# Three units of a recurrent mixer emitted side by side in slots, instead of one chain after another

## The chip, the cores and the metric

The kernel runs on one core of one Trainium2 chip. The metric is the device time of one execution in microseconds (us); smaller is better. Engines are named as the profile names them: PE is the matrix engine (PEld its weight loads), DVE the vector engine, ACT the scalar engine, POOL the GpSimd engine, SP the engine whose queue issues nearly all DMAs. L990 is line 990 of the kernel before; in the changed kernel the same statements stand some lines earlier.

## The reference, cut to what matters

One transformer layer over 256 latent tokens and 256 context tokens of width 2048: a SwiGLU block, a token mixer, a second SwiGLU block, each followed by a layer norm. The change is in the mixer alone. Half of the mixer is a gated MLP over 128-token chunks; the other half is a delta-rule recurrence, run in both directions over 16 heads of 64 channels:

```python
p_x = h_x @ w_in; p_c = h_c @ w_in
def step(s, inp):                       # per token, per head; s is 64 x 64
    r_t, v_t, w_t, k_t, a_t, b_t = inp
    sa = einsum('bhvk,bhk->bhv', s, a_t)
    s = s * w_t + sa[..., None] * b_t + v_t[..., None] * k_t
    return s, einsum('bhvk,bhk->bhv', s, r_t)
y = group_norm(ys[0] + ys[1]); out = (y + bonus) * g
out_x = concatenate([out, gmlp_mix(gm_x)]) @ w_out
```

## The kernel before, in words

**Units.** The recurrence is cut into 16 units: eight row tiles `t` of two heads each (128 channels), times two directions `d`. Each unit has 512 tokens in eight chunks of 64. Inside a chunk the recurrence is turned into small matrix products: `prep` builds decays and masked 64x64 products, `small_inverse` and `inverse` invert a triangular matrix per head and chunk, and `solve` applies the inverse and then walks the eight chunks in series: each step is two products `pS` (L1020), one DVE update `S` (L1023), and for the last four chunks two products `py` (L1010) and one DVE addition (L1011).

**Three calls per unit.** The loop calls `finish(u)` (that is `solve`, L930 to L1024, and a group norm), then `inverse(u + 1)` (L860 to L924), then for every second unit `epilogue`, then `begin(u + 2)` (`prologue` for a new row tile, `prep`, `small_inverse`, and `bonus`). No unit needs another one's result, apart from tiles that both directions of a row tile share: the three calls of one turn of the loop are independent of each other, but each stands in the program behind the one before it.

**The broadcast.** `small_inverse` puts 16x16 blocks into `a16` (eight DVE instructions, L842), writes them to DRAM (`scr`, L846), reads them back spread over the partitions (`abc`, 1 MB, L848), and then runs 15 dependent pairs of a product (`a<-x,abc`, L855) and a sum (`x<-a`, L856) on DVE. Both DMAs are issued on SP, whose queue also carries all weight loads.

**The filler.** The large products (`gemm`, `gmlp_v`, `wout`; L309 to L311, three matmuls per step of 128 channels) do not depend on the unit in hand. They stand in a `queue` of generators. `tick(w)` and `pad(w)`, called behind the small products, add `w * pace` to a debt, and once the debt has reached `BURST = 5` steps (`pad`: at once) emit large products until it is paid. `PACE` gives the weight of each place; `UNIT` is their sum over a unit, and `pace` is set per unit from the work that is left.

**What orders the instructions.** A list scheduler puts the emitted instructions into one queue per engine when the program is built: it follows the order of emission, and takes a later instruction first where its own reckoning says that the earlier one isn't ready. On the chip each of these queues is worked off in that fixed order.

Of the kernel before, what the change touches and what calls it, by code (L numbers as in the profile page):

```python
# [38 lines left out]
PACE = dict(pz=0.6, px=0.5, pt=2.8, pak=1.0, pX=0.7, pR=0.7, pu=1.1, pg=1.0, pS=0.83, rb=6, yn=0, bk=3)  # L39
# [14 lines left out]
def tile_layer(ctx: ExitStack, tc: tile.TileContext, x, c, ctx_in, c_ctx, w_ada, b_ada, ln_g, ln_b,  # L54
# [574 lines left out]
    UNIT = sum(n * PACE[k] for k, n in dict(pz=1, px=8, pt=3, pak=4, pX=8, pR=8, pu=8, pg=12, pS=6, rb=0.5, yn=0.5, bk=1).items())  # L629
# [10 lines left out]
    ahead = [0]  # L640

    def prefer(n):
        ahead[0] = n
        return tc.high_priority(offset=n) if n else nullcontext()
# [8 lines left out]
    def pad(w):  # L653

        owed[0] += w * pace[0]
        with tc.high_priority(offset=-ahead[0]) if ahead[0] else nullcontext():
            while queue and owed[0] > 0:
                owed[0] -= advance()

    def drain(gen=None):  # L660
        while queue and (gen is None or gen in queue):
            owed[0] -= advance()
        owed[0] = max(owed[0], -8.0)
# [57 lines left out]
    def prep(t, d, k, r, kk, vt, ups, kdx):  # L721
# [8 lines left out]
        tick(PACE["pz"])  # L730
# [43 lines left out]
        if d == 0:  # L774
            nc.scalar.copy(kdx, kd[:, T:W2])
        else:
            nc.gpsimd.tensor_tensor(kdx, kdx, kd[:, T:W2], op=ALU.add)

# [4 lines left out]
        for half in (1, 0):  # L783
            w = L * (1 + half)
            if half:
                pad(PACE["bk"])
            pxs = [ps_s("px") for _ in range(2)]
            for q in range(2):
                for g in range(2):
# [9 lines left out]
                    tick(PACE["px"])  # L799
# [9 lines left out]

        rhs = held("rhs", (P, 4, 2, 2, 64))  # L810
# [5 lines left out]
        tick(PACE["pt"])  # L816
        nc.scalar.copy(rhs[:, :, :, 1, :], pt.rearrange("p (g h c) -> p g h c", g=4, h=2))
        for q in range(2):
            pt = ps_s("pt")
            for g in range(4):  # L820
                nc.tensor.transpose(pt[:, P * g:P * g + P], bk[q][:, g].rearrange("p m s -> p (m s)"), ident)
            tick(PACE["pt"])
            nc.scalar.copy(fl(bkt[:, q]), pt)
        pt = ps_s("pak")
        for g in range(4):
# [5 lines left out]
            tick(PACE["pak"])  # L831
        nc.scalar.copy(rhs[:, :, :, 0, :], pt.rearrange("p (g h c) -> p g h c", g=4, h=2))
        return dict(wn=wn, rt=rt, aa=aa, arm=arm, rhs=rhs, bkt=bkt)

    def small_inverse(d, s):

        a16 = own("a16", (P, 8, 16))
        for b in range(4):
            for q in range(2):
# [9 lines left out]
                            scr.rearrange("(g s) c -> g (s c)", g=8).unsqueeze(1).to_broadcast([8, 16, 2048]))  # L849
        x = own("x16", (P, 8, 16), bufs=2)  # L850
        nc.scalar.copy(x, i16.unsqueeze(1).to_broadcast([P, 8, 16]))
        sub = own("a16", (P, 8, 16))
        for i in (range(1, 16) if d == 0 else range(14, -1, -1)):
            r = slice(0, i + 1) if d == 0 else slice(i, 16)
            nc.vector.tensor_tensor(sub[:, :, r], x[:, :, r], abc[:, r, :, i].rearrange("p s j -> p j s"), op=ALU.mult)  # L855
            nc.vector.tensor_reduce(x[:, :, i], sub[:, :, r], axis=AX.X, op=ALU.add)  # L856
        s["x16"] = x

    def inverse(d, s):

        aa = s["aa"]

# [5 lines left out]
        nc.vector.transpose(Rt, R1)  # L868
        pX = ps_v("pX")
        for i in range(8):  # L870
# [4 lines left out]
            if i % 2:  # L875
                tick(PACE["pX"])
        Z = own("Z", (P, 8, 32))
        nc.vector.tensor_tensor(Z, pX[:, 0:256].rearrange("p (i t) -> p i t", t=32),
                                ml[d].unsqueeze(1).to_broadcast([P, 8, 32]), op=ALU.mult)
        pR = ps_v("pR")  # L880
        for i in range(8):
# [3 lines left out]
            if i % 2:  # L885
                tick(PACE["pX"])
# [7 lines left out]
        fa, fb = (0, 32) if d == 0 else (32, 0)  # L894
        pX = ps_v("pX2")
        for i in range(8):
# [4 lines left out]
            if i % 2:  # L901
                tick(PACE["pR"])
        Z = own("Z", (P, 8, 32))
        for q in range(2):
# [4 lines left out]
            else:  # L909
                nc.vector.tensor_copy(Z[sb], pz)  # L910
        pR = ps_v("pR2")
        for i in range(8):
# [3 lines left out]
            if i % 2:  # L916
                tick(PACE["pR"])
# [9 lines left out]
    def solve(d, s, vt, y):  # L927
# [7 lines left out]
        for half in range(2):  # L935
            pu = ps_v("pu")
            for g in range(2):
                for h in range(2):
# [5 lines left out]
                    tick(PACE["pu"])  # L944
# [4 lines left out]
            nc.scalar.copy(uv[1][64:128, g2], puv[64:128, :, :, 0, :])  # L949

# [9 lines left out]

        pgs = [ps_v("pg") for _ in range(2)]
        pqs = [ps_v("pq"), ps_s("pq")]
        HS = [slice(64 * h, 64 * h + 64) for h in range(2)]

        def pq_at(q, g, m):
            return pqs[q][:, 128 * g + 64 * m:128 * g + 64 * m + 64]

        for g in range(4):
# [4 lines left out]
            if g >= 2:  # L973
                for q in range(2):
                    for h in range(2):
                        nc.tensor.matmul(pq_at(q, g - 2, 0)[HS[h]], ua[HS[q], g, h, :], arm[HS[q], q, h, g - 2, :],
                                         start=True, stop=True)
        tick(6 * PACE["pg"])
        for q in range(2):
# [4 lines left out]
            for g in range(2):  # L984
                for h in range(2):
                    nc.tensor.matmul(pq_at(q, g, 1)[HS[h]], uv[q][:, 2 + g, h, :], arm[:, q, h, g, :], start=True, stop=True)
            tick(3 * PACE["pg"])
        for q in range(2):
# [3 lines left out]
            for ga, gb in ([(gs[0], gs[-1] + 1)] if len(gs) == gs[-1] + 1 - gs[0] else [(0, 2), (3, 4)]):  # L992
                nc.vector.tensor_tensor(wc[:, ga:gb, q, :], pgv[:, ga:gb, 1, :],
                                        w4[:, ga:gb, q:q + 1].to_broadcast([P, gb - ga, 64]), op=ALU.mult)
        for q in range(2):
# [6 lines left out]

        S = None
        for n, cc in enumerate(order):
            g, q = cc // 2, cc % 2
            if cc >= 4:
                py = ps_v("py")
                for h in range(2):
                    hs = slice(64 * h, 64 * h + 64)
                    nc.tensor.matmul(py[hs, 0:L], S[hs, :], qt[hs, g - 2, q, :], start=True, stop=True)  # L1010
                nc.vector.tensor_tensor(yv[:, g - 2, q, :], py[:, 0:L], yl[:, g - 2, q, :], op=ALU.add)  # L1011
            if n == 7:
                break
            if S is None:
                S = wc[:, g, q, :]
                continue
            pS = ps_v("pS")
            for h in range(2):
                hs = slice(64 * h, 64 * h + 64)
                nc.tensor.matmul(pS[hs, 0:64], gi[hs, g, q, :], S[hs, :], start=True, stop=True)  # L1020
            tick(PACE["pS"])
            Sn = own("S", (P, 64), bufs=2)
            nc.vector.scalar_tensor_tensor(Sn, pS[:, 0:64], wn[:, cc:cc + 1], wc[:, g, q, :], op0=ALU.mult, op1=ALU.add)  # L1023
            S = Sn  # L1024
# [13 lines left out]
    def prologue(t):  # L1038
# [6 lines left out]
        nc.scalar.activation(sq, kkr, AF.Square)  # L1045
        pn = ps_s("pn")
# [7 lines left out]
        pad(PACE["rb"])  # L1054
# [13 lines left out]
        return dict(kk=kk, vt=vt, kdx=kdx)  # L1068
# [26 lines left out]
    def epilogue(t, y, bon):  # L1095
# [3 lines left out]
        pad(PACE["yn"])  # L1099
# [12 lines left out]
    def begin(u):  # L1112
        t, d = u // 2, u % 2
        if d == 0:
            shared[t] = prologue(t)
        sh = shared[t]
        unit[u] = prep(t, d, xs[t, 0], xs[t, 2], sh["kk"], sh["vt"], ups[t], sh["kdx"])
        if d == 1 and t + 1 < NRT:
            ups[t + 1] = load_ups(t + 1)
        small_inverse(d, unit[u])  # L1120
        if d == 1:
            bonus(t, sh)

    def finish(u):
# [3 lines left out]
        solve(d, unit.pop(u), shared[t]["vt"], yt[t])  # L1128
        if d == 1:
            group_norm(yt[t])  # L1130

# [140 lines left out]
    begin(0)  # L1272
# [4 lines left out]
    begin(1)  # L1277
    inverse(0, unit[0])
# [4 lines left out]
    for u in range(nu):  # L1283
        t, d = u // 2, u % 2
        pace[0] = left[0] / (nu - u + REST) / UNIT
# [7 lines left out]
        finish(u)  # L1293
        if u + 1 < nu:
            with prefer(OFFM):
                inverse((u + 1) % 2, unit[u + 1])
            ahead[0] = 0
        if d == 1:
            epilogue(t, yt[t], shared[t]["bon"])
        if u + 2 < nu:  # L1300
# [3 lines left out]
            with prefer(OFFB):  # L1304
                begin(u + 2)
            ahead[0] = 0
# [85 lines left out]
```

## Time and profile before

| | us |
|---|---|
| median of three runs | 3515.47 (3507.73 to 3519.03) |
| the profiled execution | 3526.16 |
| its span, first to last instruction | 3524.4 |
| PE busy in the span | 3290.2 |
| DVE busy in the span | 2174.5 |
| ACT busy in the span | 1261.3 |

The profile page gives busy time per engine, then the span in 40 slices of 88 us. The mixer's units lie in the slices in which PE falls to 7 and 8 tenths. A PE share is the time in which at least one matmul is under way, whatever the clock; the granted clock (PEclk) stands beside it. The group tables give the busy time of like instructions and the idle time of their engine just before them, with what ended it. The timeline lists an engine's instructions one after the other, with idle time in square brackets.

### The profile page before, as it was taken

The numbers are of one execution on the slowest core, as the hardware profiler recorded it, in microseconds if no ns is written. First come the engines' busy times: TensorE is split into PE (matmuls) and PEld (weight loads), VectorE is DVE, ScalarE is ACT, GpSimd is POOL, SyncE is SP. The second block draws the span as 40 slices with busy tenths as digits, with TensorE's granted clock in tenths as the row PEclk, the third lists the DMA queues.
The fourth block names the chain that finished last, engine by engine and source line by source line (L and its number), as shares of the span: only waits on it lengthen the run. The fifth ranks groups of instructions, "written<-read, shape, count | busy, mean of one in ns | idle before, by whom it ended". The sixth has DMA issues, their size and how long they took to land. (4 is left out here: it accounts for less than half of the span.)

```text
span 3524.4 us, 62262 instructions
## 1 busy us (share of the span) xinstructions
PE 3290.2 (93%) x24340; PEld 2748.6 (78%) x24340; DVE 2174.5 (62%) x4527; ACT 1261.3 (36%) x2241; POOL 453.0 (13%) x401
## 2 busy tenths in 40 slices
PE   8999999999999999998887888788888999999997
PEld 4656777777787888887865667666777999999997
DVE  3345697865655755338766665667556766666666
ACT  2322222222222222224643444344332544444443
POOL 2100000000000000004623232323213200000002
PEclk9999999999999999999898889798878999999999
DMA  8766465665654754233533343333433566566655
GB/s 297 251 206 185 144 207 161 188 223 173 213 179 150 235 168 153 91 97 116 159 85 97 82 102 82 95 92 102 117 89 101 162 184 185 185 182 184 185 182 160
DMA packets 701990, 550.58 MB, mean 156 GB/s; under 512 B 24139, under 2 KB 624368, under 8 KB 699648
## 3 DMA queue, kind: packets, MB, share of 16 engines
q1 hardware_dynamic: 701248, 546.40, 51.7%
q8 instruction: 192, 3.15, 0.4%
q14 instruction: 102, 0.84, 0.1%
q0 software_dynamic: 384, 0.17, 0.0%
q10 hardware_dynamic: 64, 0.02, 0.0%
HBM read 539.16 MB, written 7.34 MB: 155 GB/s over the span
## 5 line engine op out<-in xcount | busy, mean ns | idle before, releaser
L297 ACT CAST whi<-raw 128x512 fp32r<-128x512 f32 (+1 forms) x1366 | 839.2, 617 | 1773.4 <-PE po L310 487.3
L300 DVE TENSOR_TENSOR wlo<-raw,whi 128x512 fp32r<-128x512 f32 (+1 forms) x1196 | 832.2, 698 | 605.2 <-ACT whi L297 584.3
L300 POOL TENSOR_TENSOR wlo<-raw,whi 128x512 fp32r<-128x512 f32 x170 | 232.6, 1371 | 2681.4 <-ACT whi L297 2649.3
L309 PE MATMUL po<-ahi,whi 128*128 128x256 f32 (+1 forms) x1472 | 491.7, 334 | 2.9 <-DVE X L415 2.2
L311 PE MATMUL po<-ahi,wlo 128*128 128x256 f32 (+1 forms) x1472 | 488.9, 332 | 5.0 <-DVE wlo L300 5.0
L310 PE MATMUL po<-alo,whi 128*128 128x256 f32 (+1 forms) x1472 | 490.7, 333 | 0.7 <-DVE alo L306 0.7
L309 PE MATMUL pgate<-h,whi 128*128 128x512 f32 (+1 forms) x1408 | 478.0, 339 | 5.6 <-ACT h L305 4.5
L309 PE MATMUL pup<-h,whi 128*128 128x512 f32 (+1 forms) x1408 | 477.9, 339 | 0.6 <-ACT whi L297 0.6
L311 PE MATMUL pgate<-h,wlo 128*128 128x512 f32 (+1 forms) x1408 | 475.3, 338 | 1.7 <-DVE wlo L300 1.7
L310 PE MATMUL pgate<-h,whi 128*128 128x512 f32 (+1 forms) x1408 | 474.6, 337 | 2.2 <-DVE h L306 2.2
L311 PE MATMUL pup<-h,wlo 128*128 128x512 f32 (+1 forms) x1408 | 475.1, 337 | 1.5 <-DVE wlo L300 1.3
L310 PE MATMUL pup<-h,whi 128*128 128x512 f32 (+1 forms) x1408 | 474.0, 337 | 0.0
L309 PEld LDWEIGHTS pgate<-h,whi 128*128 128x128 f32 x1408 | 267.4, 190 | 57.8 <-ACT whi L297 13.0
L309 PEld LDWEIGHTS po<-ahi,whi 128*128 128x128 f32 x1472 | 278.4, 189 | 42.8 <-issue 7.2
L309 PEld LDWEIGHTS pup<-h,whi 128*128 128x128 f32 x1408 | 267.4, 190 | 51.7 <-ACT whi L297 13.9
L310 PEld LDWEIGHTS po<-alo,whi 128*128 128x128 f32 x1472 | 278.6, 189 | 36.0 <-issue 7.5
L311 PEld LDWEIGHTS po<-ahi,wlo 128*128 128x128 f32 x1472 | 278.7, 189 | 34.8 <-DVE wlo L300 5.8
L311 PEld LDWEIGHTS pup<-h,wlo 128*128 128x128 f32 x1408 | 267.1, 190 | 33.5 <-DVE wlo L300 4.1
L310 PEld LDWEIGHTS pgate<-h,whi 128*128 128x128 f32 x1408 | 267.4, 190 | 32.8 <-DVE h L306 3.3
L311 PEld LDWEIGHTS pgate<-h,wlo 128*128 128x128 f32 x1408 | 267.3, 190 | 32.5 <-DVE wlo L300 3.9
L310 PEld LDWEIGHTS pup<-h,whi 128*128 128x128 f32 x1408 | 267.2, 190 | 28.1 <-issue 1.7
L415 DVE SCALAR_TENSOR_TENSOR X<-po,modc,X 128x256 f32<-128x256 f32 x352 | 155.1, 479 | 154.1 <-PE po L311 149.1
(352 smaller groups left out, 4788.4 us busy)
## 6 DMA issues: line engine op xcount, KB each, us to landing
raw<-in_ffn_b_wi_dram SPq DMA_DIRECT2D x164, 512.0 KB, 4.1
raw<-in_ffn_a_wi_dram SPq DMA_DIRECT2D x156, 512.0 KB, 4.2
xv<-in_w_ada_dram SPq DMA_DIRECT2D x256, 256.0 KB, 3.5
xk<-in_w_ada_dram SPq DMA_DIRECT2D x256, 256.0 KB, 3.8
raw<-in_w_in_dram SPq DMA_DIRECT2D x110, 512.0 KB, 3.8
raw<-in_ffn_a_wo_dram SPq DMA_DIRECT2D x96, 512.0 KB, 3.5
raw<-in_ffn_b_wo_dram SPq DMA_DIRECT2D x88, 512.0 KB, 3.3
abc<-scr SPq DMA_DIRECT2D x16, 1024.0 KB
```

The source lines that it names most:

```text
L297: nc.scalar.copy(hi, r)
L300: (nc.gpsimd if turn[1] and turn[0] % turn[1] == 0 else nc.vector).tensor_tensor(lo, r, hi.bitcast(F32), op=ALU.subtract)
L309: nc.tensor.matmul(o, wh, ah, start=start, stop=False)
L310: nc.tensor.matmul(o, wh, al, start=False, stop=False)
L311: nc.tensor.matmul(o, wl, ah, start=False, stop=stop)
L415: nc.vector.scalar_tensor_tensor(xs, po[:, sl], gc[:, d:d + 1], xs, op0=ALU.mult, op1=ALU.add)
```

## The change

`finish`, `inverse` and `begin` become generators that yield at places where a result has to come back from another engine. A new function `together` advances the three (for units `u`, `u + 1`, `u + 2`) by one piece each, in that order, and then calls `burst`, which pays the whole debt of large products at once; such a turn is a slot. All calls of `tick` and `pad` and the table `PACE` go. `pace` is now the number of steps per slot, the work that is left divided by the units left and by `SLOTS = 13`.

```diff
-PACE = dict(pz=0.6, px=0.5, pt=2.8, pak=1.0, pX=0.7, pR=0.7, pu=1.1, pg=1.0, pS=0.83, rb=6, yn=0, bk=3)
+SLOTS = 13
-    def tick(w):
-        owed[0] += w * pace[0]
-        if owed[0] >= BURST:
-            with tc.high_priority(offset=-ahead[0]) if ahead[0] else nullcontext():
-                while queue and owed[0] > 0:
-                    owed[0] -= advance()
+    def burst():
+        owed[0] += pace[0]
+        while queue and owed[0] > 0:
+            owed[0] -= advance()
...
+    def together(*chains):
+        chains = list(chains)
+        while chains:
+            for ch in list(chains):
+                if next(ch, chains) is chains:
+                    chains.remove(ch)
+            burst()
...
-        finish(u)
+        chains = [finish(u)]
         if u + 1 < nu:
-            with prefer(OFFM):
-                inverse((u + 1) % 2, unit[u + 1])
-            ahead[0] = 0
-        if d == 1:
-            epilogue(t, yt[t], shared[t]["bon"])
+            chains.append(inverse((u + 1) % 2, unit[u + 1]))
         if u + 2 < nu:
             if d == 0:
                 for i in range(3):
                     drain(gens[t + 1, i])
-            with prefer(OFFB):
-                begin(u + 2)
-            ahead[0] = 0
+            chains.append(begin(u + 2))
+        together(*chains)
+        if u + 2 < nu:
+            begun(u + 2)
```

`begun` emits the `a16` blocks, the two DMAs of the broadcast and, for the second direction, `bonus`. The 15 pairs of DVE steps behind the broadcast move out of `small_inverse` into the start of `inverse`, one turn of the loop later, with a yield after every third:

```diff
+        return small_steps(d, s, abc)
+    def small_steps(d, s, abc):
...
             nc.vector.tensor_tensor(sub[:, :, r], x[:, :, r], abc[:, r, :, i].rearrange("p s j -> p j s"), op=ALU.mult)
             nc.vector.tensor_reduce(x[:, :, i], sub[:, :, r], axis=AX.X, op=ALU.add)
+            if i % 3 == 0:
+                yield
...
     def inverse(d, s):
         aa = s["aa"]
+        yield
+        yield from s["small"]
```

In `solve` the products `pq` come behind `pg` and its two DVE results instead of among them, with a slot between; and each step of the walk emits `pS`, `py`, then the DVE update `S`, then the addition of `y`:

```diff
-        S = None
-        for n, cc in enumerate(order):
+        S = wc[:, order[0] // 2, order[0] % 2, :]
+        for n, cc in enumerate(order[1:], 1):
+            yield
+            if n < 7:
+                pS = ps_v("pS")
+                for h in range(2):
+                    nc.tensor.matmul(pS[HS[h], 0:64], gi[HS[h], g, q, :], S[HS[h], :], start=True, stop=True)
...
+            if n < 7:
+                Sn = own("S", (P, 64), bufs=2)
+                nc.vector.scalar_tensor_tensor(Sn, pS[:, 0:64], wn[:, cc:cc + 1], wc[:, g, q, :], op0=ALU.mult, op1=ALU.add)
```

The yields make 10 slots of a `finish` in the first direction and 12 in the second, 11 of an `inverse`, and 11 or 8 of a `begin`. The numbers of instructions on PE are the same in both programs, 20411 matmuls; what differs is their order. Three places show it.

**DVE, start of unit 4 (first direction), before.** `gi` and `wc` are what the first `pS` needs; `a` and `x` are the steps behind the broadcast `abc`; `a<-aa` are the blocks that the broadcast carries; `wlo` belongs to the large products.

```order
L842 SCALAR_TENSOR_TENSOR a_17439<-aa,mb,a_17439 64x128 x6
L672 SCALAR_TENSOR_TENSOR xv<-pp,mus,xv 128x192
L1077 TENSOR_TENSOR bon<-pb,xv 128x256
L672 SCALAR_TENSOR_TENSOR xv<-pp,mus,xv 128x192
L300 TENSOR_TENSOR wlo<-raw,whi 128x512 x3
L990 TENSOR_TENSOR gi<-pg,i_93 128x4x64
L993 TENSOR_TENSOR wc<-pg,wn 128x4x64
L997 TENSOR_TENSOR qy<-pq,ra 128x2x64
L855 TENSOR_TENSOR a_17454<-x_17452,abc 128x8x2
L990 TENSOR_TENSOR gi<-pg,i_93 128x4x64
L856 TENSOR_REDUCE x_17452<-a_17454 128x8
L993 TENSOR_TENSOR wc<-pg,wn 128x3x64
```

The first step on the broadcast stands ten instructions behind the block that it carries, and ahead of the second `gi`.

**DVE, start of unit 4, now.** Between the last block of this broadcast and the first step on it stand 26 rows, and twelve more between that step and the first row shown.

```order
L844 TENSOR_TENSOR a_17669<-x_17667,abc 128x8x8
L845 TENSOR_REDUCE x_17667<-a_17669 128x8
L844 TENSOR_TENSOR a_17669<-x_17667,abc 128x8x9
L300 TENSOR_TENSOR wlo<-raw,whi 128x512
L845 TENSOR_REDUCE x_17667<-a_17669 128x8
L963 TENSOR_TENSOR gi<-pg,i_93 128x4x64
L966 TENSOR_TENSOR wc<-pg,wn 128x4x64
L963 TENSOR_TENSOR gi<-pg,i_93 128x4x64
L966 TENSOR_TENSOR wc<-pg,wn 128x3x64
L844 TENSOR_TENSOR a_17669<-x_17667,abc 128x8x10
```

Eight of the 15 steps now stand ahead of `gi`; `gi` and `wc` stand together. (In units of the second direction two steps stand ahead of `gi`, as in the next fence.)

**DVE, start of unit 3 (second direction), now.** The same names; the last block of the broadcast is the first row.

```order
L828 SCALAR_TENSOR_TENSOR a_16896<-aa,mb,a_16896 64x128
L300 TENSOR_TENSOR wlo<-raw,whi 128x512
L912 COPY R<-pR_16852 32x8x32
L300 TENSOR_TENSOR wlo<-raw,whi 128x512
L722 SCALAR_TENSOR_TENSOR nb<-ic,kk 128x512
L724 TENSOR_REDUCE zp<-zp 128x8
L726 SCALAR_TENSOR_TENSOR pf<-m_96,zp 128x520
L844 TENSOR_TENSOR a_17039<-x_17037,abc 128x8x2
L845 TENSOR_REDUCE x_17037<-a_17039 128x8
L844 TENSOR_TENSOR a_17039<-x_17037,abc 128x8x3
L963 TENSOR_TENSOR gi<-pg,i_93 128x4x64
```

Six instructions lie between the last block and the first step here, and one of them (`nb`) needs products of the new unit's first slot.

**PE, end of unit 4, before.** `pX` and `pR` are products of the inverse, `pp` large products.

```order
L309 MATMUL pp<-h_13088,whi 128x512
L310 MATMUL pp<-h_13089,whi 128x512
L311 MATMUL pp<-h_13088,wlo 128x512
L873 MATMUL pX<-Rt,aa 32x32 x32
L309 MATMUL pp<-h_13096,whi 128x512
L310 MATMUL pp<-h_13097,whi 128x512
L311 MATMUL pp<-h_13096,wlo 128x512
L309 MATMUL pp<-h_13148,whi 128x512
L884 MATMUL pR<-R_17104,Z 32x32 x32
```

**PE, second half of unit 4, now.** `px`, `pt` and `pak` are products of `prep`.

```order
L784 MATMUL px<-ar,bk_17820 128x128 x3
L784 MATMUL px<-ar,bk_17821 128x128 x4
L995 MATMUL pS<-S,gi 64x64 x2
L999 MATMUL py<-qy,S 64x64 x2
L866 MATMUL pX<-Rt,aa 32x32 x32
L784 MATMUL px<-ac,bk_17820 64x64 x8
L784 MATMUL px<-ac,bk_17821 64x64 x8
L995 MATMUL pS<-S,gi 64x64 x2
L999 MATMUL py<-qy,S 64x64 x2
L876 MATMUL pR<-R_17931,Z 32x32 x32
L802 MATMUL pt<-ident,ac 128x128 x2
L802 MATMUL pt<-ident,ar 128x128 x2
```

Products of three units now alternate; in this stretch of a unit of the first direction no large product stands among them.

## Rows read from the trace of the kernel before

**Rows 1.** The profile page: span, busy time, slices of 88 us.
```profile
span 3524.4 us, 62262 instructions
PE 3290.2 (93%) x24340; PEld 2748.6 (78%) x24340; DVE 2174.5 (62%) x4527; ACT 1261.3 (36%) x2241; POOL 453.0 (13%) x401
PE   8999999999999999998887888788888999999997
```
**Rows 2.** Windows: start and end, length, busy time by engine, granted clock, DMA.
```profile
1740.00:1810.70 70.70, 54.10 (x677) 45.74 (x675) 49.52 (x132) 25.84 (x49) 19.57 (x18) 0.84 0.41 96
1810.70:2676.00 865.30, 724.66 (x9155) 589.45 (x9155) 538.67 (x1618) 339.16 (x633) 246.68 (x212) 0.85 0.37 94
```
**Rows 3.** PE groups by form, 1795 to 2690: busy, mean ns, idle before.
```profile
L1020 PE MATMUL pS<-wc,gi 64*64 64x64 f32 x64 | 7.2, 317 | 60.0 <-DVE gi L990 27.5 <-DVE x L856 19.6 <-DVE a L855 13.0
L1020 PE MATMUL pS<-S,gi 64*64 64x64 f32 x320 | 27.7, 254 | 10.0 <-DVE S L1023 10.0
L797 PE MATMUL px<-ar,bk 64*128 64x128 f32 x224 | 24.8, 346 | 11.1 <-POOL bk L773 11.1
L899 PE MATMUL pX<-Rt,aa 32*32 32x32 f32 x512 | 12.7, 200 | 4.9 <-DVE Rt L890 4.7
L873 PE MATMUL pX<-Rt,aa 32*32 32x32 f32 x960 | 12.5, 199 | 8.6 <-DVE Rt L868 8.1 <-DVE gst L1157 0.5
L884 PE MATMUL pR<-R,Z 32*32 32x32 f32 x960 | 12.3, 200 | 5.7 <-DVE Z L878 3.2 <-issue 2.5
```
**Rows 4.** Waits of DVE, 1795 to 2690: total, times, longest.
```profile
DVE a L855 <- DMA abc<-scr: 98.6, 14, 13.8
```
**Rows 5.** DVE in order of time, start of unit 4.
```profile
2017.66 2.25 DVE L842 SCALAR_TENSOR_TENSOR a<-aa,mb,a 64x128 f32<-64x128 f32 x6
...
2035.57 0.18 DVE L855 TENSOR_TENSOR a<-x,abc 128x16 f32<-128x16 f32 x1 [5.91 <-DMA abc<-scr]
2035.67 0.42 DVE L990 TENSOR_TENSOR gi<-pg,i 128x256 f32<-128x256 f32 x1
```
**Rows 6.** PE in order of time, the same stretch.
```profile
2030.96 0.28 PE L310 MATMUL pgv<-wlo,h 128*128 128x256 f32 x1
2031.08 0.28 PE L311 MATMUL pgv<-whi,h 128*128 128x256 f32 x1
2036.14 0.48 PE L1020 MATMUL pS<-wc,gi 64*64 64x64 f32 x4 [4.79 <-DVE gi L990]
...
2036.93 0.41 PE L310 MATMUL pgv<-wlo,h 128*128 128x256 f32 x1
2037.14 0.41 PE L311 MATMUL pgv<-whi,h 128*128 128x256 f32 x1
```
**Rows 7.** Windows of a few us: unit 4 before and after its wait, and unit 11.
```profile
2024.00:2031.00 7.00, 7.00 (x93) 6.72 (x93) 3.59 (x5) 4.60 (x8) 4.55 (x3) 1.00 0.69 151
2036.60:2047.10 10.50, 8.80 (x44) 7.02 (x42) 7.60 (x23) 3.97 (x8) 3.82 (x3) 0.50 0.48 143
2465.20:2470.30 5.10, 4.16 (x93) 3.27 (x94) 3.18 (x8) 2.46 (x5) 1.47 (x2) 1.00 0.10 25
2470.30:2477.10 6.80, 6.80 (x52) 5.30 (x50) 4.82 (x14) 2.99 (x5) 2.19 (x3) 0.50 0.16 50
```
**Rows 8.** DVE groups by form, 1795 to 2690.
```profile
L1023 DVE SCALAR_TENSOR_TENSOR S<-pS,wn,wc 128x64 f32<-128x64 f32 x96 | 26.6, 277 | 23.2 <-PE pS L1020 23.0
L808 DVE TENSOR_TENSOR aa<-px,ma 128x256 f32<-128x256 f32 x56 | 21.9, 417 | 7.4 <-PE px L797 7.3
L855 DVE TENSOR_TENSOR a<-x,abc 128x104 f32<-128x104 f32 x15 | 8.0, 534 | 0.1
L855 DVE TENSOR_TENSOR a<-x,abc 128x128 f32<-128x128 f32 x15 | 6.2, 415 | 0.1
```
**Rows 9.** POOL groups by form, 1795 to 2690.
```profile
L773 POOL TENSOR_TENSOR bk<-kd,ei 128x256 f32<-128x256 f32 x28 | 23.3, 854 | 30.3 <-DVE kd L770 24.9 <-ACT R L922 3.5 <-ACT whi L297 1.9
L758 POOL TENSOR_TENSOR ar<-kk,e 128x256 f32<-128x256 f32 x14 | 11.5, 819 | 28.8 <-ACT e L744 28.2 <-DVE wlo L300 0.6
```

More of the change, by code (lines that the diff above doesn't have):

```diff
@@ L777, in prep @@
             nc.gpsimd.tensor_tensor(kdx, kdx, kd[:, T:W2], op=ALU.add)
+        for _ in range(3):
+            yield
         aa = held("aa", (P, 2, 2, 4, L))
@@ L784, in prep @@
             w = L * (1 + half)
-            if half:
-                pad(PACE["bk"])
+            if not half:
+                yield
             pxs = [ps_s("px") for _ in range(2)]
@@ L959, in solve @@
         yv = y.rearrange("p (g q t) -> p g q t", g=2, q=2)
+        HS = [slice(64 * h, 64 * h + 64) for h in range(2)]
         pgs = [ps_v("pg") for _ in range(2)]
[L962 to L966, printed above, removed]
         for g in range(4):
@@ L972, in solve @@
                                      start=True, stop=True)
[L973 to L978, printed above, removed]
         for q in range(2):
@@ L994, in solve @@
                                         w4[:, ga:gb, q:q + 1].to_broadcast([P, gb - ga, 64]), op=ALU.mult)
+        yield
+        pqs = [ps_v("pq") for _ in range(2)]
+        for g in range(2):
+            for q in range(2):
+                for h in range(2):
+                    nc.tensor.matmul(pqs[q][HS[h], 128 * g:128 * g + 64], ua[HS[q], 2 + g, h, :], arm[HS[q], q, h, g, :],
+                                     start=True, stop=True)
+        for q in range(2):
+            for g in range(2):
+                for h in range(2):
+                    nc.tensor.matmul(pqs[q][HS[h], 128 * g + 64:128 * g + 128], uv[q][:, 2 + g, h, :], arm[:, q, h, g, :],
+                                     start=True, stop=True)
         for q in range(2):
@@ L1114, in begin, with begun @@
         if d == 0:
-            shared[t] = prologue(t)
+            shared[t] = {}
+            yield from prologue(t, shared[t])
         sh = shared[t]
-        unit[u] = prep(t, d, xs[t, 0], xs[t, 2], sh["kk"], sh["vt"], ups[t], sh["kdx"])
+        unit[u] = {}
+        yield from prep(t, d, xs[t, 0], xs[t, 2], sh["kk"], sh["vt"], ups[t], sh["kdx"], unit[u])
+        yield
+    def begun(u):
+        t, d = u // 2, u % 2
         if d == 1 and t + 1 < NRT:
             ups[t + 1] = load_ups(t + 1)
-        small_inverse(d, unit[u])
+        unit[u]["small"] = small_inverse(d, unit[u])
         if d == 1:
-            bonus(t, sh)
+            bonus(t, shared[t])
     def finish(u):
@@ L1127, in finish @@
             yt[t] = own("y", (P, T))
-        solve(d, unit.pop(u), shared[t]["vt"], yt[t])
+        yield from solve(d, unit[u], shared[t]["vt"], yt[t])
         if d == 1:
+            yield
             group_norm(yt[t])
+            yield
+            epilogue(t, yt[t], shared[t]["bon"])
+    def together(*chains):
[5 more added lines that the diff above has]
+            burst()
     ub = 3 * RW + 2 * P
@@ L1271, in tile_layer @@
     ups[0] = load_ups(0)
-    begin(0)
+    pace[0] = BURST
+    together(begin(0))
+    begun(0)
     left[0] = 1032
@@ L1276, in tile_layer @@
     gens[1, 2] = put(project(1, 2))
-    begin(1)
-    inverse(0, unit[0])
+    together(inverse(0, unit[0]), begin(1))
+    begun(1)
     gm = []
@@ L1284, in tile_layer @@
         t, d = u // 2, u % 2
-        pace[0] = left[0] / (nu - u + REST) / UNIT
+        pace[0] = left[0] / (nu - u + REST) / SLOTS
         if t + 2 < NRT:
```

71 lines of the change are left out of this document (21 added, 50 removed).

## The prediction

> **What bounds the kernel now.** I read the page first. PE is under way 93% of the span, but its slices fall to 7 and 8 tenths in the middle, and only there [rows 1]: the mixer. The rest of the program is the same instructions in the same order, so I count it as unchanged.
>
> The windows cut the mixer out. From the first `pS` of unit 0 to the first `pS` of unit 15 it takes 865.3 us, 57.7 us per unit [rows 2]. PE is busy 724.7 us of it, so 140.6 us are idle. The granted clock is 0.85; as it has two levels, 1.2 and 2.4 GHz, this is 30% of the stretch, 260 us, at 1.2. If all the idle time lies inside those 260 us, the lower clock costs half of the other 119, 60 us; if none does, it costs 130. So idle time and clock together hold 200 to 270 us, and PE's own work at 2.4 GHz is 595 to 665 us, 40 to 44 us per unit. DVE is busy 538.7 us, 36 us per unit [rows 2]: it is no bound by its sum, but by its order.
>
> That order is the next thing to see. Of PE's idle time 60.0 us stand before one group, the first `pS` of a unit, ended by `gi`, `x` and `a` on DVE [rows 3]. The waits of DVE say why: the first step on the broadcast waited 14 times for its DMA, 98.6 us [rows 4]. Unit 4 shows both at once. The blocks of the broadcast end at 2019.91; the second `gi` stands in DVE's queue behind the step that reads the broadcast; DVE sits still for 5.91 us until 2035.57, 15.7 us after the blocks; only then comes `gi` [rows 5]. PE has run out of large products at 2031 and starts `pS` at 2036.14 [rows 6]. After it the clock is 0.50 for 10.5 us, where it had been 1.00 [rows 7], and the same large product follows the one before it after 0.21 us [rows 6]. So one late DMA is paid three times: DVE, PE, clock.
>
> **The change, part by part.**
>
> *The wait for the broadcast.* The first step moves away from the DMA it waits for, behind the slots of the next turn of the loop. In units of the first direction 26 rows of DVE now lie between the last block and the first step, which is several slots of PE; with 57.7 us over 13 slots a slot is about 4.4 us, so the 15.7 us of the broadcast are over in four. There nothing should wait. In units of the second direction six rows lie between, and one of these needs products of the new unit: two or three slots, 9 to 13 us. There 3 to 7 us of DVE waiting can remain, but `gi` is now followed by a burst, `pq`, and another burst before the first `pS`, where before `pS` came behind one burst; a burst of 15 products with 256 columns is at least 15 x 0.12 = 1.8 us (0.12 from 2030.96 to 2031.08, [rows 6]). I take 50 of the 60.0 us as gone. Bounds: 0 and 60.
>
> *The clock behind it.* The wait is 60.0 of 140.6 us, 43% of the idle time; 43% of 60 to 130 us is 26 to 56. The row of unit 4 gives 8.80 busy us at half clock, 4.4 us for one wait; with 12 such waits 53. I take the middle, 41, and of it 50/60: 34 us. Bounds: 0 and 56.
>
> *Inverse and walk side by side.* Before, `pX`, `pR` and so on come in series behind the walk, each waiting for DVE with little between; the groups `pX`, `pR` and the later `pS` wait 8.6 + 4.9 + 5.7 + 10.0 = 29.2 us [rows 3]. Now each round trip of one chain runs beside two other chains and a burst of 12 to 15 products. I take half as gone, 15 us. Bounds: 0 and 29.
>
> *What is new.* In seven units of the first direction a `pS` follows 16 `px` directly, and on DVE its `S` stands behind the masks of these `px`: two `aa` and `S` are 2 x 0.417 + 0.277 = 1.1 us [rows 8], 8 us in all. If all six masks of a unit and `Z` stood ahead, it would be 3.2 us, 22 us in all. I take 10. `px` still waits for POOL's `bk` (11.1 us [rows 3]); DVE and POOL do the same work as before, so I take 0, with 11 us either way. The broadcast's DMAs keep their place in SP's queue among the weight loads, which follow the bursts; a load is issued when its buffer comes free, and the 15.7 us already contain this. The start (70.7 us [rows 2]) and the end of the mixer have the same chain with nothing beside it: 0.
>
> Sum: -50 - 34 - 15 + 10 = -89 us. The profiled execution took 3526.2 us, 1.8 us more than its span, so 3437 by its own scale. It lies 10.7 us above the median of 3515.5; on the median's scale the forecast is **3426 us**. The terms' bounds, the small ends and the large ends together, give 3515 - 156 and 3515 + 33; as all ends seldom meet, its own range is 3370 to 3497.
>
> **A rule that speaks against it.** The `a<-x,abc` with 104 elements takes 534 ns on average, the one with 128 takes 415 [rows 8]: a shorter instruction is longer, so something else holds some of them up. POOL is busy 246.7 us in the stretch [rows 2], among it `bk`, `ar` and `ac` of `prep`. The Trainium skill (SBUF — State Buffer, section "Who interferes with whom") says that a DVE instruction with two SBUF inputs and a GpSimd instruction that reads SBUF exclude each other for a whole instruction. The trace agrees in direction (534 against 415 ns); it doesn't show which instruction held which.
>
> **Rivals.**
>
> 1. *DVE and POOL hold each other up.* Side by side, the steps on the broadcast (two SBUF inputs) run while `prep` has POOL busy, which before came later. If every `bk` and `ar` (23.3 + 11.5 us [rows 9]) and as much again for the other POOL operations of a unit were added to DVE on the path, 47 us would be given back: 3473 us. Against it: DVE has 22 us per unit to spare. The rule above is this case.
>
> 2. *The interleaving hides nearly everything.* Idle time falls from 140 to 50 us and the clock rises to 0.95. Then 90 us of idle time go and about 60 to 85 of the clock's loss: 150 to 175, 3340 to 3365 us. For it: 12 to 15 large products now stand between almost any two steps of a chain, on paper enough for 0.3 us of DVE. Against it: the chain `pu`, `pg`, `gi`, `pq`, `qy`, `pS` has the same length as before.
>
> 3. *The wait only moves.* The first step on the broadcast still stands ahead of `gi`, eight steps ahead of it in units of the first direction. If the broadcast lands later than I reckon, since denser bursts draw more weight loads ahead of it, DVE waits again, and `gi` with it, now with eight steps more to do first. Then the gain of 15 is met by such steps: 3505 to 3526.
>
> 4. *Slower: the clock falls in the runs of small products.* In half of the units there is now a run of some twelve rows of small products, `px`, `pS`, `pX`, `pR`, `pt`, without a large one. Such a run exists before: 93 small matmuls in 5.1 us, PE busy 4.16, clock 1.00; and in the next 6.8 us, PE busy throughout, it is 0.50 [rows 7]. Such a fall costs 3.4 us. Without the clock term I gain 55 us, so one more fall per unit (16 x 3.4 = 54) is the point from which it decides; two more per unit give -55 + 109 = +54, 3570 us. Against it: 0.9 us of idle time lie in that run too, and behind the long wait of unit 4 the fall was longer, so idle time seems the larger cause, and that is what the change takes away.
>
> **How the numbers follow.** Forecast 0.58; rival 1 0.10; rival 2 0.10; rival 3 0.09; rival 4 0.13. Within 0.3%, 3505 to 3526, is about what a measurement of this kernel can't tell from no change. Faster than that: 0.58 + 0.10 + 0.10 and a part of rival 3, 0.80; within it 0.07; slower 0.13. The range of 3360 to 3510 leaves out most of rivals 2 and 4 and holds the rest.
>
> **What would show it.** Right: the 60 us before the first `pS` of a unit fall under 15; DVE's wait for the broadcast falls from 98.6 to under 40, what is left lying in every second unit; the clock of the stretch rises from 0.85 to 0.90 or more; a unit takes about 52 us. Wrong: `gi` still waits behind `a<-x,abc`; or `pS` waits for `S` more than 30 us in all; or the clock stays at 0.85 with less idle time, which would be rival 4; or `a<-x,abc` grows beyond 0.5 us on average, rival 1.

## The result and the profile after

| | before | changed | ratio, 95% interval |
|---|---|---|---|
| median, us | 3514.64 (3507.73 to 3519.03) | 3452.69 (3451.90 to 3456.67) | 0.9828 [0.981, 0.9846] |
| profiled execution, us | 3526.16 | 3452.98 | |

The change gains 62 us, 1.7%, and its interval lies clear of no change; the forecast was 89. The page of the changed kernel answers to [rows 1]: span, busy time, PE's slices.

```profile
span 3451.0 us, 62280 instructions
PE 3228.4 (94%) x24340; PEld 2713.6 (79%) x24340; DVE 2187.8 (63%) x4527; ACT 1254.8 (36%) x2241; POOL 448.2 (13%) x401
PE   8999999999999999999888878788888999999997
```

Each engine's instructions are the same in number, and the slices of the mixer are hardly fuller than before. So the gain is not where I looked for it. To see where it is I cut the mixer at the same two events in both kernels, from the first `pz` to the last `pgt`. First the window of before and what follows it to the end of the program, then the same of the changed kernel and a part of its window; columns as in [rows 2].

```profile
1731.10:2689.10 958.00, 799.24 (x10001) 653.20 (x10000) 601.60 (x1790) 376.81 (x701) 275.05 (x236) 0.85 0.37 94
2689.10:3524.40 835.30, 803.25 (x6627) 797.44 (x6625) 543.55 (x907) 386.37 (x679) 60.15 (x50) 0.98 0.58 176
```

```profile
1728.50:2623.70 895.20, 745.88 (x10046) 625.48 (x10044) 621.02 (x1797) 373.03 (x706) 271.87 (x237) 0.89 0.39 102
2623.70:3451.00 827.30, 796.15 (x6582) 790.39 (x6581) 538.91 (x900) 383.41 (x674) 58.86 (x48) 0.98 0.59 176
1820.70:2603.10 782.40, 650.04 (x9052) 542.93 (x9051) 545.43 (x1596) 326.87 (x623) 237.40 (x208) 0.89 0.39 101
```

The stretch is 62.8 us shorter. Length less PE busy is idle time: 958.0 - 799.2 = 158.8 before and 895.2 - 745.9 = 149.3 after, only 9.5 less. The time at 1.2 GHz is twice the missing share of the clock: 2 x 0.15 x 958 = 287 before, 2 x 0.11 x 895 = 197 after. With the unrounded clock and the idle time inside the slow stretches taken out (53.7 of 279.9 us, 49.8 of 191.1), half of the rest is lost, as an estimate: 113 us before, 71 after, 42 less. That leaves 11 us, for which these rows name no cause: the changed kernel even has 45 more matmuls in this stretch, which before stood behind it (6627 against 6582 in the second rows). So of the 62.8 us between these two executions two thirds are clock and a sixth idle time.

The gain of the medians, 62 us, need not divide in the same way. The span fell by 73.4 us: 62.8 here, 8.0 behind the stretch, where those 45 products are gone, and 2.6 ahead of it. The profiled execution of before is 10.7 us above its median, and its granted clock over the whole span is 0.952; among the executions of that kernel that ran beside the first experiments the longest (3523.29 us) had 0.953 and the shortest (3507.86 us) 0.957. So some of the 42 us are probably this one execution's; if all 10.7 are, the clock holds some 32 of the median's 62, a half. That is an estimate; no pair of executions at their medians has a trace.

The last row is unit 0 to unit 15, from first `pS` to first `pS`: 782.4 / 15 = 52.2 us per unit, as forecast. It is 82.9 us shorter than in [rows 2], near the 89 that were summed up for it, but 9052 matmuls stand in it instead of 9155: large products have moved to the two ends of the mixer, which take 958.0 - 865.3 = 92.7 us before and 895.2 - 782.4 = 112.8 now. The prediction had put the ends at 0.

One of the four executions of the kernel with the early broadcast, below, took 8011.61 us at a granted clock of 1.0; it is left out of that ratio, and the record doesn't show what held it up.

The waits of PE (total, times, longest) and the groups that answer to [rows 3], of the changed kernel over the whole stretch; then DVE's wait that answers to [rows 4], over the whole stretch before and now:

```profile
PE pq L973 <- DVE wc L966: 54.8, 9, 9.4
PE pgb L1084 <- DVE y L1075: 24.1, 8, 9.7
PE px L784 <- POOL bk L758: 11.6, 13, 3.6
```

```profile
L995 PE MATMUL pS<-wc,gi 64*64 64x64 f32 x64 | 5.8, 261 | 0.0
L995 PE MATMUL pS<-S,gi 64*64 64x64 f32 x320 | 28.5, 249 | 4.9 <-DVE S L1002 4.0 <-ACT ic L720 0.9
L876 PE MATMUL pR<-R,Z 32*32 32x32 f32 x1024 | 12.9, 200 | 6.4 <-DVE Z L869 5.4 <-issue 1.0
L866 PE MATMUL pX<-Rt,aa 32*32 32x32 f32 x1024 | 13.6, 198 | 2.3 <-DVE Rt L860 2.2
L890 PE MATMUL pX<-Rt,aa 32*32 32x32 f32 x512 | 11.5, 195 | 2.5 <-DVE Rt L880 2.5
```

```profile
DVE a L855 <- DMA abc<-scr: 100.7, 15, 13.8
DVE a L844 <- DMA abc<-scr: 105.9, 15, 10.3
```

The first `pS` of a unit waits for nothing any more: 60.0 has become 0.0, which alone would look like success. But DVE waits for the broadcast as long as ever, 105.9 us against 100.7 (98.6 in [rows 4], which start later), and PE has a wait of 54.8 us one product earlier, at `pq`, and one of 24.1 at the group norm's `pgb`, where there had been 1.5. One unit shows why, unit 5, of the second direction. DVE in order of time; `a<-aa` is the last block of the broadcast.

```profile
2050.64 0.35 DVE L828 SCALAR_TENSOR_TENSOR a<-aa,mb,a 64x128 f32<-64x128 f32 x1
...
2055.33 1.38 DVE L657 SCALAR_TENSOR_TENSOR xk<-pp,mus,xk 128x252 f32<-128x252 f32 x3
2065.91 0.18 DVE L844 TENSOR_TENSOR a<-x,abc 128x16 f32<-128x16 f32 x1 [9.21 <-DMA abc<-scr]
...
2068.76 0.42 DVE L963 TENSOR_TENSOR gi<-pg,i 128x256 f32<-128x256 f32 x1
```

PE in the same stretch, and the windows around its wait:

```profile
2062.33 0.44 PE L973 MATMUL pq<-ra,ua 64*64 64x64 f32 x6
2072.18 0.69 PE L973 MATMUL pq<-ra,ua 64*64 64x64 f32 x10 [9.40 <-DVE wc L966]
```

```profile
2050.99:2065.73 14.74, 11.79 (x181) 9.87 (x179) 3.69 (x8) 7.17 (x16) 2.57 (x2) 0.98 0.70 123
2062.77:2072.18 9.41, 0.01 (x2) 0.03 (x1) 6.15 (x18) 2.27 (x5) 1.62 (x2) 0.63 0.48 91
2072.18:2082.20 10.02, 10.02 (x67) 8.66 (x68) 6.21 (x24) 4.13 (x8) 4.74 (x6) 0.50 0.10 28
```

From the block to the first step 14.9 us pass, as in [rows 5] (15.7). In them DVE is busy 3.69 us and then stands still for 9.21, with `gi` and `wc` behind it in its queue although the `pg` that they read ended at 2060.4. PE issues the first `pq` and then has nothing for 9.4 us: `pq` takes its PSUM buffers over from `pg`, so it can't go on until `gi` and `wc` have read `pg` (the run with another PSUM buffer, below, bears this out). In the first 3.1 of these 9.4 us DVE still stands; then it is busy, 6.15 us, with what stands ahead of the last `wc`, and with `gi` and `wc` themselves. Then PE runs 10.0 us at 1.2 GHz. The late DMA is still paid three times; only the name of the product that pays it has changed.

All turns together show the same. In the nine waits before `pq`, 54.8 us, DVE stands for the DMA in 8.3 us only; in most of the rest it works off the steps on the broadcast (16.9), `pf` (8.2), `gi` (4.4) and `wc` (4.1). So PE pays for the work that stands ahead of `gi` and `wc` more than for the standing. Of the 225 steps that could stand ahead of the last `gi` of the unit in hand, 139 do now; before it was 66. In the second direction it is 2 to 10 of a unit's 15, not two as in the one unit listed ahead.

Whether DVE waits at a turn depends on the work between block and step, not on the rows. Unit 4, whose 26 rows the prediction counted, is the only turn without a wait: DVE is busy 11.16 us in between. Unit 6, first direction too, has 4.64 us of work and waits. Their windows from block to step, then the two steps:

```profile
1991.62:2009.26 17.64, 16.50 (x228) 14.96 (x230) 11.16 (x35) 6.13 (x11) 5.96 (x5) 0.81 0.68 169
2097.07:2113.16 16.09, 8.61 (x158) 6.55 (x158) 4.64 (x21) 1.97 (x4) 2.87 (x3) 0.89 0.57 117
```

```profile
2009.26 0.55 DVE L844 TENSOR_TENSOR a<-x,abc 128x16 f32<-128x16 f32 x1
2113.16 0.18 DVE L844 TENSOR_TENSOR a<-x,abc 128x16 f32<-128x16 f32 x1 [8.54 <-DMA abc<-scr]
```

The other seven turns of the first direction have 2.9 to 7.4 us of work and wait 4.2 to 10.4 us, 51.8 in all; the turns of the second direction wait 52.5, and the first broadcast, ahead of all turns, 1.6.

### The profile page after: what moved, and what is told of

The parts are those of the page before. It is cut to its first block, busy times and chain, and to the rows that moved or that the text cites. A ratio compares the mean times of both kernels' runs of the same rounds, so it can differ in the third digit from the quotient of the medians.

```text
span 3451.0 us, 62280 instructions
## 1 busy us (share of the span) xinstructions
PE 3228.4 (94%) x24340; PEld 2713.6 (79%) x24340; DVE 2187.8 (63%) x4527; ACT 1254.8 (36%) x2241; POOL 448.2 (13%) x401
```

## The experiments

Each gives its ratio to the kernel before, which ran beside it on the same chip. Where an expectation speaks of theory A, it is this: DVE's queue stands at the first step on the broadcast, and everything behind it waits.

**Hold the steps back until `wc` stands.** The steps start from a copy of a constant into `x`. A zero made out of the last `wc` of the unit in hand becomes the bias of this copy, so that no scheduler can put the steps ahead of it.

```diff
+        zc = own("zc", (P, 1))
+        nc.vector.tensor_scalar(zc, wc[:, order[0] // 2, 1, 0:1], 0.0, None, op0=ALU.mult)
+        held_back[0] = zc
...
-        nc.scalar.copy(x, i16.unsqueeze(1).to_broadcast([P, 8, 16]))
+        if held_back[0] is None:
+            nc.scalar.copy(x, i16.unsqueeze(1).to_broadcast([P, 8, 16]))
+        else:
+            nc.scalar.activation(x, i16.unsqueeze(1).to_broadcast([P, 8, 16]), AF.Identity, scale=1.0, bias=held_back[0])
```

> The changed kernel, with one edit: the first of the 15 steps on the broadcast may start only when gi and wc of the unit in hand stand (its start value is copied with a bias of 0 that is worked out from wc). No step can then hold up gi and wc. Theory A (the idle time of PE that is left hangs on DVE standing still for the broadcast ahead of gi): PE's wait before pq (54.8 us) falls under 10, PE's idle time in the mixer from 149 to about 95, DVE's wait for the broadcast from 106 to under 50; the clock's loss falls with it, 40 to 80 us faster, 3375 to 3415. Theory B (the wait before pq is the length of the chain pu, pg, gi, wc itself): it stays at 40 or more, and the time is within 10 us of 3453. Theory C (the inverse is the longest chain of a turn, and holding it back lengthens the turn): waits before pX and pR grow by as much as pq loses, no gain.

Measured: 3400.03 us, ratio 0.9677 [0.9657, 0.9698], another 53 us below the changed kernel; it is the fastest of all, level with one variant below. Its waits of PE and its mixer:

```profile
PE px L784 <- POOL bk L758: 19.6, 11, 3.7
PE pq L981 <- DVE wc L971: 11.4, 4, 5.5
PE pgb L1092 <- DVE y L1083: 6.4, 8, 1.6
```

```profile
1726.80:2565.70 838.90, 735.24 (x10047) 612.93 (x10045) 624.00 (x1813) 378.13 (x709) 272.03 (x237) 0.93 0.41 108
```

One small DVE instruction per unit, and a bias in a copy that was there already, take 54.8 to 11.4 and 24.1 to 6.4, and idle time from 149.3 to 103.7. No step stands ahead of `gi` any more, and DVE's wait for the broadcast is down to 5.4 us. I also counted PE's idle time that lies inside DVE's waits for the broadcast or in the 4 us behind each: 74.5 us before, 67.1 in the changed kernel, 1.1 here. The theory holds, though idle time was to fall to 95 and `pq` under 10: two waits grew (`px` on `bk` from 11.6 to 19.6, `pX` on `Rt` from 2.2 to 9.7), and 20 of the 66 us of idle time came back elsewhere.

**Start the broadcast earlier.** Its blocks and DMAs are emitted in `prep`, right behind the masks that they read, and the steps get another buffer for their scratch.

```diff
         yield
+        s["aa"] = aa
+        s["small"] = small_inverse(d, s)
...
-        sub = own("a16", (P, 8, 16))
+        sub = own("Z", (P, 8, 32))
...
-        unit[u]["small"] = small_inverse(d, unit[u])
```

> The changed kernel, with the blocks of the broadcast and its two DMAs emitted in prep directly behind the masks of px, one to four slots earlier than behind the turn; the steps' scratch moves to another buffer so that the blocks need not wait for the steps before. Theory A: each DMA starts some 4 to 8 us earlier against gi, DVE's wait for the broadcast falls from 106 to 30 to 60 us, PE's wait before pq from 55 to 15 to 30, and the one before pgb (24 us) to under 12; 20 to 50 us faster, 3400 to 3430. Theory B (the wait before pq is the chain itself): 3453 within 10 us.

Measured: 3442.58 us, ratio 0.9797 [0.9778, 0.9815].

```profile
PE pq L975 <- DVE wc L968: 57.7, 11, 8.5
DVE Z L846 <- DMA abc<-scr: 51.1, 10, 8.3
```

DVE's wait halves as expected, but `pq` waits as long as before and the time misses what was expected: 10 us are gained, not 20 to 50. 163 of the 225 steps stand ahead of `gi` here, and in the waits before `pq` DVE never stands for the DMA: it works. The order has to be mended, not the landing.

**Give `pq` another PSUM buffer.**

```diff
-        pqs = [ps_v("pq") for _ in range(2)]
+        pqs = [ps_s("pq") for _ in range(2)]
```

> The changed kernel, with the two PSUM buffers of pq taken from the other pool, so that pq need not wait until gi and wc have read the buffers of pg. Theory A (DVE is late; PSUM is only the place where PE notices it): the wait before pq falls under 10 us, and one of about the same size, less the 1.5 us of pq and one burst per unit, stands before the first pS or before the products that need the other pool; the time moves by less than 20 us. Rival (the PSUM buffers are the cause): the wait goes and stays away, 40 us or more faster, 3410 or less.

Measured: 3462.62 us, ratio 0.9857 [0.9842, 0.9873].

```profile
PE pS L995 <- DVE wc L966: 41.7, 7, 8.6
DVE a L844 <- DMA abc<-scr: 101.2, 15, 10.7
```

The wait before `pq` is gone, and 41.7 us of it stand at the first `pS`, where it was before the change; the time is 10 us longer, not shorter. PSUM was the place where PE noticed, not the cause.

**Emit the steps four slots later.**

```diff
         aa = s["aa"]
-        yield
+        for _ in range(4):
+            yield
         yield from s["small"]
```

> The changed kernel with four more yields ahead of the steps on the broadcast, so that the program emits them some four slots (about 17 us) later. If the place of emission decides when the steps run (rival), they stand behind gi and wc of the unit in hand, as when they were held back by a result: wait of pq for wc under 20 us, DVE's wait for the broadcast under 40 us, time 3400 to 3420. If the list scheduler decides it by its own reckoning of when the broadcast has landed (theory A), the steps still stand ahead of gi, in most units 10 to 15 of them: the waits of PE for gi and wc stay at 50 us or more in all, DVE's wait for the broadcast may fall because other work is put ahead of it, and the time is 3440 to 3475.

Measured: 3460.14 us, ratio 0.985 [0.9824, 0.9877].

```profile
PE pu L309 <- ACT wsT L1185: 27.1, 4, 8.8
PE pR L906 <- DVE Z L900: 19.6, 6, 9.5
PE pq L974 <- DVE wc L967: 7.5, 5, 2.7
```

```profile
DVE a L844 <- DMA abc<-scr: 98.9, 15, 10.6
```

The time and DVE's wait are as theory A has them, but a number it gave is missed: the waits for `gi` and `wc` fell to 7.5, not stayed above 50. Since PE's idle time inside and just behind DVE's waits is 74.1 us here, the wait has only got other names again: 20.6 of the 27.1 us of `pu` and 17.5 of the 19.6 of `pR` lie there. In 14 of 15 units the scheduler placed ten or more steps ahead of the last `gi`, 190 of 225 in all, although the program emits them later.

**Pay the large products after each chain, not after all three.**

```diff
+            n = len(chains)
             for ch in list(chains):
                 if next(ch, chains) is chains:
                     chains.remove(ch)
-            burst()
+                burst(1.0 / n)
```

> The changed kernel, with the large products of a slot paid in equal parts behind each of the two or three chains instead of in one burst at its end. Theory D (most of the change's gain is the clock: large products in one piece bring it back after a gap and keep it): the loss by the clock goes from 71 back towards 113 us, time 3475 to 3500. Rival E (the gain is of the chains standing side by side, the burst's form does nothing): 3453 within 12 us, the time at the lower clock stays near 190 us.

Measured: 3463.83 us, ratio 0.9861 [0.9843, 0.9879], 11 us slower than the changed kernel. Its mixer:

```profile
1728.40:2632.90 904.50, 754.85 (x10047) 620.88 (x10045) 621.52 (x1797) 373.16 (x706) 268.72 (x237) 0.89 0.40 101
```

The clock is 0.89 as in the changed kernel. The one burst per slot is not what brought the clock back; it is worth some 11 us.

**The changed code, one chain after the other.** Each chain gets slots and bursts of its own; `SLOTS` becomes 32, since a unit now has about that many, so the bursts are smaller too.

```diff
-SLOTS = 13
+SLOTS = 32
...
-        chains = [finish(u)]
+        together(finish(u))
...
-            chains.append(inverse((u + 1) % 2, unit[u + 1]))
+            together(inverse((u + 1) % 2, unit[u + 1]))
...
-            chains.append(begin(u + 2))
-        together(*chains)
+            together(begin(u + 2))
```

> The changed code with its slots, but finish, inverse and begin of a turn emitted one after the other again, each in slots of its own; SLOTS is 32 instead of 13, so that a turn still pays about the same number of large products, now some 6 per slot. Theory E (the gain of the change is that three chains share each round trip): most of the gain goes, 3500 to 3540, with the time at the lower clock back at 250 us or more. Theory F (the gain is of the new order inside the walk, S ahead of y, and of pq behind gi and wc): 3453 within 15 us.

Measured: 3517.07 us, ratio 1.0003 [0.9986, 1.002]. The time at 1.2 GHz is 242 us, a little under the 250 expected.

```profile
1728.20:2672.50 944.30, 790.65 (x9988) 643.06 (x9987) 628.58 (x1787) 377.31 (x703) 271.70 (x235) 0.87 0.37 95
```

```profile
PE py L999 <- DVE S L1002: 20.2, 5, 5.9
PE pq L973 <- DVE wc L966: 19.6, 3, 10.8
PE pX L866 <- DVE Rt L860: 17.4, 10, 3.6
PE pS L995 <- DVE S L1002: 16.5, 4, 6.5
```

No gain is left. The new order of `pq`, the moved steps and the slots give nothing by themselves; it takes three chains side by side. The smaller bursts are changed along with them here; cutting a burst in three cost 11 us above, so they can hardly be all of it. The round trip of `pX` in [rows 3] is back (17.4 us). The waits of `py` and `pS` for `S` are mostly the broadcast again: the steps now stand behind `gi` in 13 of 15 units and ahead of `S`, and 16.8 of the 20.2 us and 12.3 of the 16.5 lie inside DVE's waits for the DMA.

**The kernel before, with the steps held back.** They move to the start of `inverse` and get the same zero.

```diff
         aa = s["aa"]
+        small_steps(d, s)
```

> The kernel before, with only the steps on the broadcast moved to the start of inverse and held back until gi and wc of the unit in hand stand, as in the gated kernel. Theory A (the broadcast's wait in front of gi was the largest single loss already before): PE's wait before the first pS (60 us) falls under 15; the time falls by 40 to 90 us, 3425 to 3475. Rival (before, the steps were hidden behind the wait, and now lengthen the serial chain walk, steps, inverse): the waits before pX rise by 40 us or more and the time is 3500 or more.

Measured: 3507.22 us, ratio 0.9982 [0.9966, 0.9997].

```profile
L1033 PE MATMUL pS<-wc,gi 64*64 64x64 f32 x64 | 5.4, 248 | 3.2 <-DVE wc L1003 3.2
```

```profile
PE pS L1033 <- DVE S L1036: 33.9, 9, 7.1
PE px L797 <- POOL bk L773: 21.3, 16, 4.5
DVE a L865 <- issue: 29.9, 5, 7.9
DVE a L865 <- DMA abc<-scr: 22.9, 4, 7.0
```

```profile
1728.90:2679.70 950.80, 796.77 (x10001) 652.25 (x10000) 618.40 (x1806) 377.13 (x702) 266.80 (x236) 0.86 0.38 95
```

The wait before the first `pS` goes, 60.0 to 3.2, as expected; the time misses what was expected by far: 9 us. Idle time is 950.8 - 796.8 = 154.0, against 158.8. The later `pS` now wait 33.9 for `S` (10.0 in [rows 3]), and this is the broadcast once more: DVE still sits idle 52.8 us before the first step, and 24.7 of the 33.9 us lie inside its waits. For 29.9 of the 52.8 the profile names no releaser, but these steps too begin 15.5 to 18.6 us after the last block, those with the DMA named 14.3 to 16.1. In the held-back kernel with three chains the first step comes 14.3 to 33.7 us after the block and waits for the DMA 5.4 us in all. That behind `wc` no other chain's work delays the steps here is the likely reason; no run isolates it. The rival of the expectation has the time right, not the reason: `pX` waits 11.6 + 7.6 us, not 40 more. Held back alone -9, side by side alone -62, both -115: 44 us more than the sum.

**Three variants of the held-back kernel.** First, with the early broadcast too (the edits of the first two experiments together):

> The gated kernel with the blocks and DMAs of the broadcast emitted behind the masks of px, as in the run with early DMAs. If the DMA still limits the steps once they are held back, the waits before pX (9.7 us) go and 5 to 20 us are gained against 3400; if holding back has already given the DMA its time, 3400 within 10 us, or some us worse, since the blocks then stand ahead of S on DVE.

Measured: 3404.46 us, 0.9701 [0.9675, 0.9727], within the noise of 3400. Once the steps stand behind `wc` and other chains run beside them, an earlier start of the broadcast gains nothing. Then two sizes of burst:

```diff
-SLOTS = 13
+SLOTS = 11
```

> The gated kernel with SLOTS 11 instead of 13, nearer to the 10 to 12 slots that a turn has, so that every burst is a fifth longer and less is left for the end. If the bursts are still too short to cover the round trips, idle time falls by 10 us or more and the time is 3380 to 3392; if they cover them already, 3400 within 8 us.

Measured: 3407.65 us, 0.9709 [0.9686, 0.9732].

```diff
-SLOTS = 13
+SLOTS = 15
```

> The kernel with the steps held back until wc stands (3400 us at SLOTS 13, 3408 at 11), with SLOTS = 15: smaller bursts of large products in every slot, so that the queue of large products lasts longer. If the size of a burst decides little (theory A says that what was lost stood behind the broadcast): within 10 us of 3400. If smaller bursts leave the round trips of the chains uncovered (rival): 3415 or more, with more waits of pS and pX.

Measured: 3400.27 us, 0.9677 [0.9653, 0.97], the same as with 13. The burst's size decides little.

## Why the prediction was partly right

**The wait for the broadcast (-50): wrong, and the main term.** The step that failed is "Between the last block and the first step 26 rows of DVE now lie, which is several slots of PE", from which it followed that in the first direction "nothing should wait". Rows of one engine's queue are not time on another. It held for unit 4, where the rows were counted; the other seven turns of the first direction have 2.9 to 7.4 us of work on DVE between block and step, against the 13 to 16 us of the broadcast, and wait 51.8 us, as much as the second direction. I took the order of emission, four slots, for the time of execution. Emitting the steps later (3460 us) shows that it isn't; making them depend on `wc` (3400 us) shows what was missing. Idle time of the mixer fell by 9.5 us, not 50. Of the marks I had set, the 60 us before the first `pS` did go and a unit takes 52 us; but DVE's wait did not fall under 40, the clock stopped at 0.89, and "`gi` still waits behind `a<-x,abc`" came true. The first two marks could come true while the term was wrong, since they don't see a wait that changes its name.

**Rival 3, the wait only moves, had the mechanism** ("DVE waits again, and `gi` with it, now with eight steps more to do first") but neither its reason nor its price. The broadcast did not land later: where DVE waited for it, it took 13.0 to 16.2 us from the last block, against 13.0 to 18.8 before. And it gave 3505 to 3526, since it let the clock stay.

**The clock (-34): measured -42 between the profiled executions, for another reason.** I derived it from the wait that would go. The wait stayed and the clock rose all the same, 0.85 to 0.89: that this term came out near its size is luck. In the same code with the chains in series it is 0.87 (in the shortest of that kernel's ten executions, while the 0.85 is of one of before that lies above its median); with the bursts split it is still 0.89. So it comes with three chains side by side. What in them keeps the clock up is not settled: gaps of PE over 2 us fell only from 24 (112 us) to 19 (108 us).

**Inverse and walk side by side (-15): right.** The groups that waited 29.2 us in [rows 3] now wait 2.3 + 2.5 + 6.4 + 4.9 = 16.1, in a stretch that starts somewhat earlier.

**What is new (+10): wrong.** `pS` waits for `S` less than before, 4.0 us, not more. What is new is that `pgb` lost 24.1 us behind the same step on the broadcast as `pq`, in 14.1 of which DVE stood for the DMA; I had not listed the group norm among what stands behind it.

**Rival 2**, idle time of 50 us, did not come: 149.3, and 103.7 even in the best kernel. **Rival 4** is ruled out as a whole, since the clock rose, but what it described does happen: at 1836.5, 1993.5 and 2310.9 the clock fell, and in the 6.8 us ahead of each PE was busy 5.67, 4.70 and 5.03 us, with no long wait, among small products (`pS`, `py`, `pX`, `px`, `pR`) and some large ones. **Rival 1** did not come. The steps on the broadcast, busy time of the products of all 240 in the stretch before and now; then their duration in the changed kernel, minimum/median/maximum in ns, and the group of [rows 8] that had 534:

```profile
1731.10:2689.10 958.00, 88.65 (x240) 0.00 (x0) 0.85 0.37 94
1728.50:2623.70 895.20, 88.81 (x240) 0.00 (x0) 0.89 0.39 102
```

```profile
L844 DVE TENSOR_TENSOR a<-x,abc x240: 184/300/1480, 1764.1 to 2578.0; 128x16 f32<-128x16 f32 x8, 128x32 f32<-128x32 f32 x8, 128x48 f32<-128x48 f32 x8, 128x64 f32<-128x64 f32 x8
```

```profile
L844 DVE TENSOR_TENSOR a<-x,abc 128x104 f32<-128x104 f32 x16 | 6.3, 396 | 0.2
```

The total has not changed, 88.65 and 88.81 us. Single steps take up to 1480 ns (1423 before), and the mean of this form fell. Such outliers would fit the rule of the Trainium skill (SBUF — State Buffer, "Who interferes with whom"), but no run here shows which instruction held which. The price of this rival doesn't follow from its words either: 23.3 + 11.5 us and as much again are 70 us, not 47.

In the sum of 89 the terms of idle time came to -50 - 15 + 10 = -55, and -9.5 was measured; the clock gave -42 instead of -34, and -11 came from a term that the sum didn't have. That the time still fell inside the range is in good part luck: the largest term was wrong, and the clock did not need it.

## What to carry to other kernels

In these traces an instruction that waits for a DMA blocks whatever stands behind it in its engine's queue (9.21 us in the unit shown), and code that emitted it later did not move it: the list scheduler placed it ahead of `gi` all the same. Why it does so, by its reckoning of the landing perhaps, no run shows. If an instruction must come later, make it depend on what must come first. When a wait disappears from one product, look for the same microseconds under another name (here `pS`, `pq`, `pgb`, `pu`, `pR`) before calling them gone; the waiting engine's own total (100.7 to 105.9 us) tells at once. The same edit that held the steps back gained 53 us with three chains side by side and 9 with the chains in series, where the wait had only moved on to `S`.

## What was not expected of the hardware

From the issue of the 64 KB write to DRAM to the first step that could use the 1 MB read back, 14.9 us passed in the unit shown (2051.01 to 2065.91), with DMA engines 70% busy. In the unit of [rows 5] it was 15.7 us from the last block. And a wait of 9.4 us on PE was followed by 10.0 us of uninterrupted work at 1.2 GHz: as an estimate, half of these 10.0, its price is 5 us more than the wait itself.
